# Fewer transposes for the up-projection: four quarters of the sample's rows are transposed, and the four operand sums are formed on the transposed quarters

## The chip, the cores and the metric

The kernel runs on one core of one Trainium2 chip. The metric is the device time of one execution in microseconds; lower is better. Engines are named as the profile names them: PE (TensorE matmul), PEld (its weight load), DVE (VectorE), ACT (ScalarE), POOL (GpSimd) and SP (SyncE, which issues the DMAs). SBUF is the on-chip memory, and PSUM the banks that PE writes its results to.

## What is computed

One encoder layer runs for a prompt of 512 rows and a sample of 1024 rows, with a model width of 1024 and shared weights. The change lies between the output projection and the up-projection of the feed-forward part:

```python
x = x + concat(attention, conv) @ w_out
h = rmsnorm(x, norm_ffn_g)              # (1024, 1024) for the sample
u = dwconv(h @ w_up, ffn_dw_w, ffn_dw_b)  # w_up: (1024, 5632)
x = x + (silu(u[..., :2816]) * u[..., 2816:]) @ w_down
return rmsnorm(x, norm_final_g)
```

## The kernel before

**Seven products.** The sample's up-projection `h @ w_up` is cut into a left and a right half of the model width (L, R), two halves of the rows (t = 0 and 1, 512 rows each) and 22 blocks of columns j. Each j is computed by a scheme of seven products in place of eight. A product is a sum over four chunks c of 128 model dimensions, and a chunk is three matmuls of 128x512, since every fp32 operand is split into a high part (a rounded cast, made by ACT) and a low part (the difference, made by DVE or POOL). In `prod` these are the lines 1194, 1195 (low part of the operand) and 1196 (low part of the weight). The weights' sums and splits are `sums_up` and `split_up` (line 1180, with POOL at line 1074).

**Seven operands.** With e for the rows of t = 0 and x for those of t = 1, the operands on the side of the rows are, by number: 1 is e's left half, 2 is e's right half, 4 is x's right half, 5 is s1 = xL + xR, 6 is s2 = s1 - eL, 7 is eL - xL, and 3 is eR - s2. PE needs them with the model dimensions along the partitions, so rows have to be transposed.

**Rows, sums, transposes.** `scaled(i)` multiplies a finished block of 128 rows by its norm and forms the sums on rows, with DVE. `turned(i, get)` then transposes an operand: for each chunk it takes a bank, runs four transposes of 128x128 (line 1125, one for each block of rows b), casts the high part on ACT (line 1127) and subtracts for the low part on DVE (lines 1128 and 1074). Seven operands of four chunks make 28 banks and 112 transposes. Operands 1 and 2 (32 transposes, banks named "u") are made while the output projection still runs. Operands 4, 6, 7, 5 and 3 (80 transposes) use four banks named "t".

**Order.** PE's order is written by hand from here on (`tc.manual_schedule`); DVE, ACT and POOL are ordered by the scheduler, and each engine executes its list in order. `every(n, gen)` advances the generator of transposes between the chunks of a product, so transposes stand between matmuls in `second(0)`, `fourth(0)` and `second(1)`. A bank "t" is used again when DVE has read it. When the transposes are through, the four banks "t" are given back as two wide banks, "w2" and "w3", for the products' other sums: `armed` writes a throwaway matmul into each (line 1260), ACT copies a first product over it (line 1394), and `sixth(0)` accumulates onto it. Then follow `sixth(1)`, `seventh(0)`, `seventh(1)`, `fifth` and `third`, and the other blocks.

Of the kernel before, what the change touches and what calls it, by code (L numbers as in the profile page):

```python
# [15 lines left out]
P = 128  # L16
D = 1024
# [91 lines left out]
def tile_hybrid_encoder(ctx: ExitStack, tc: tile.TileContext, xs, rel_bias, norm_attn_g, w_in,  # L109
# [981 lines left out]
    def scaled(i):  # L1091
# [3 lines left out]
        if t == 0:  # L1095
            nc.vector.scalar_tensor_tensor(x[:], x1[i][:], rs2[:, i:i + 1], gFb[:], op0=ALU.mult, op1=ALU.mult)
            x1.pop(i)
            return
        for s in (R, L):
            nc.vector.scalar_tensor_tensor(x[:, s], x1[i][:, s], rs2[:, i:i + 1], gFb[:, s], op0=ALU.mult, op1=ALU.mult)  # L1100
        x1.pop(i)
        e = rows[0, b]
        s1 = rows["s1", b] = sb.tile([NT])
        s2 = rows["s2", b] = sb.tile([NT])
        add(s1[:], x[:, L], x[:, R])
        sub(s2[:], s1[:], e[:, L])
        sub(x[:, L], e[:, L], x[:, L])
        if i >= NB - 2:
            last_sum(b)

    def last_sum(b):
        sub(rows[0, b][:, L], rows[0, b][:, R], rows["s2", b][:])

    def block_rows(i, b):
        if i in (1, 2, 3):
            return rows[0, b][:, R if i == 2 else L]
        if i in (4, 7):
            return rows[1, b][:, R if i == 4 else L]
        return rows["s1" if i == 5 else "s2", b][:]

    def turned(i, get):
        for c in range(4):
            held, ap = get()
            for b in range(4):
                nc.tensor.transpose(ap[:, b * P:(b + 1) * P], block_rows(i, b)[:, c * P:(c + 1) * P], ident[:])
            hi, lo = A[i, c] = (sb.tile([NT], F32R), sb.tile([NT], F32R))
            nc.scalar.copy(hi[:], ap)
            sub(lo[:], ap, hi[:].bitcast(F32))
            held = None
            yield 0.0  # L1130
        key = {6: "s2", 5: "s1", 7: 1, 3: 0}.get(i)
        for b in range(4):
            rows.pop((key, b), None)
# [88 lines left out]
    for b in range(2):  # L1222
        last_sum(b)
# [146 lines left out]
    turns = chain(*(turned(i, turn_bank) for i in (4, 6, 7, 5, 3)))  # L1370
# [7 lines left out]
    second(0, every(7, turns))  # L1378
    fourth(0, every(7, turns), True)
    second(1, chain(every(8, turns)))  # L1380
    for _ in turns:
        raise RuntimeError("turns left")
    pt_guard.__exit__(None, None, None)
# [24 lines left out]
    sixth(1)  # L1408
    split_up(1, 3)
# [420 lines left out]
```

## Time and profile before

| what | value |
|---|---|
| median of 3 runs | 1485.77 us (1485.22 to 1486.96) |
| the profiled execution | 1484.85 us, span of its instructions 1483.1 us |
| PE busy | 1468.5 us of the span, 99% |
| DVE, ACT, POOL busy | 1118.2, 805.5 and 770.7 us |
| transposes of `turned` into "u" | 32, from 693.8 to 727.7 us |
| transposes of `turned` into "t" | 80, from 737.8 to 753.3 us |
| first matmul of `sixth(0)` | 757.88 us |

All times of rows are microseconds from the start of the span. A row of the timeline gives start, duration, engine, line, operation, output and inputs by the program's names with numbers left out (w<-h,q), shape and count, and in brackets how long the engine was idle before and what it waited for. Records of matmuls that follow each other overlap; the distance from start to start is what one costs. A group counts as busy from its first start to its last end.

### The profile page before, as it was taken

What the parts mean: (1) busy time and instruction counts of PE and PEld (TensorE: products, weight loads), DVE (VectorE), ACT (ScalarE), POOL (GpSimd) and SP (SyncE); (2) the same over time, 40 slices, a digit from 0 to 9 for tenths busy, and PEclk for the clock granted to TensorE, in tenths of its full rate; (3) what the DMA queues carried; (4) which work ended last, traced back from release to release, by engine and by line L of the source; (5) the groups of instructions that cost most, each with busy time, mean ns of one, the idle gap of its engine ahead of it and who ended that gap; (6) DMA issues with size and microseconds to landing.
All of it is one profiled execution on the core that took longest, in us unless ns stands there. A gap on an engine that the chain in (4) does not pass through costs nothing.

```text
span 1483.1 us, 19870 instructions
## 1 busy us (share of the span) xinstructions
PE 1468.5 (99%) x6736; PEld 1212.0 (82%) x6736; DVE 1118.2 (75%) x1510; ACT 805.5 (54%) x1424; POOL 770.7 (52%) x689
## 2 busy tenths in 40 slices
PE   9999999999999999999999999999999999999998
PEld 7788887878888888788888888888888888888886
DVE  6877945648988888676868888888886856578774
ACT  7524555567778776653465545445544553433355
POOL 3564453338779766322336666666654251135546
PEclk9999999999999999999999999999999999999999
DMA  9554331844444454663214443333332494356644
GB/s 367 200 151 146 102 107 29 263 142 142 127 137 136 134 178 142 201 225 108 71 58 142 135 135 128 127 130 128 123 126 87 152 326 167 124 188 220 224 163 163
DMA packets 124626, 228.19 MB, mean 154 GB/s; under 512 B 20420, under 2 KB 45764, under 8 KB 124397
## 3 DMA queue, kind: packets, MB, share of 16 engines
q1 hardware_dynamic: 124092, 226.37, 46.6%
q8 instruction: 53, 0.87, 0.2%
q10 hardware_dynamic: 432, 0.56, 0.1%
q14 instruction: 49, 0.39, 0.1%
HBM read 166.83 MB, written 61.10 MB: 154 GB/s over the span
## 4 chain that ended last, share of the span: by engine, by line
PE 89%; DVE 3%; DMA 3%; ACT 2%; POOL 2%; issue 1%; SPq 0%; POOLq 0%; DVEq 0%; ACTq 0%
PE w L1194 8%; PE w L1196 8%; PE w L1195 8%; PE w L1528 7%; PE w L1527 7%; PE w L1526 7%; PE b L315 4%; PE b L317 4%; PE b L316 4%; PE u L315 4%; PE u L317 4%; PE u L316 4%; PE a L692 1%; PE a L650 1%; PE u L796 1%; PE u L798 1%
## 5 line engine op out<-in xcount | busy, mean ns | idle before, releaser
L163 POOL TENSOR_TENSOR q<-q,q 128x1024 fp32r<-128x1024 f32 x66 | 159.2, 2412 | 66.9 <-ACT q L162 42.8
L1074 POOL TENSOR_TENSOR q<-q,q 128x512 fp32r<-128x512 f32 x81 | 116.5, 1445 | 119.4 <-ACT q L1180 117.1
L1074 DVE TENSOR_TENSOR h<-h,h 128x512 fp32r<-128x512 f32 (+1 forms) x152 | 131.9, 897 | 57.6 <-ACT h L1082 23.4
L1526 PE MATMUL w<-h,h 128*128 128x512 f32 x432 | 168.0, 389 | 0.0
L1528 PE MATMUL w<-h,h 128*128 128x512 f32 x432 | 168.0, 389 | 0.0
L1527 PE MATMUL w<-h,h 128*128 128x512 f32 x412 | 160.3, 389 | 0.0
L1194 PE MATMUL w<-h,q 128*128 128x512 f32 x368 | 144.3, 392 | 0.7 <-ACT w L1267 0.4
L1196 PE MATMUL w<-h,q 128*128 128x512 f32 x368 | 143.2, 389 | 0.0
L1195 PE MATMUL w<-h,q 128*128 128x512 f32 x347 | 135.0, 389 | 0.0
L1074 POOL TENSOR_TENSOR h<-h,h 128x512 fp32r<-128x512 f32 (+1 forms) x38 | 53.5, 1411 | 142.4 <-ACT h L1509 117.5
L1082 ACT CAST h<-h 128x512 fp32r<-128x512 f32 x116 | 69.3, 620 | 104.4 <-DVE h L1074 25.8
L315 PE MATMUL b<-h,q 128*128 128x512 f32 x312 | 123.0, 395 | 1.4 <-ACT h L461 0.8
L317 PE MATMUL b<-h,q 128*128 128x512 f32 x312 | 122.5, 393 | 0.0
L316 PE MATMUL b<-h,q 128*128 128x512 f32 x312 | 122.3, 392 | 0.0
L315 PE MATMUL u<-h,q 128*128 128x512 f32 x272 | 106.8, 393 | 0.0
L316 PE MATMUL u<-h,q 128*128 128x512 f32 x272 | 106.8, 393 | 0.0
L317 PE MATMUL u<-h,q 128*128 128x512 f32 x272 | 106.7, 392 | 0.0
L162 ACT CAST q<-q 128x1024 fp32r<-128x1024 f32 x66 | 69.1, 1048 | 52.1 <-PE u L316 16.8
L352 DVE SCALAR_TENSOR_TENSOR c<-d,cvw,c 128x512 f32<-128x512 f32 x128 | 96.0, 750 | 1.6
L344 POOL TENSOR_TENSOR h<-h,h 128x512 f32<-128x512 f32 x62 | 81.6, 1318 | 27.5 <-ACT h L343 23.0
L1526 PEld LDWEIGHTS w<-h,h 128*128 128x128 f32 x432 | 81.1, 188 | 16.8
L1528 PEld LDWEIGHTS w<-h,h 128*128 128x128 f32 x432 | 81.1, 188 | 16.7
(474 smaller groups left out, 3990.3 us busy)
## 6 DMA issues: line engine op xcount, KB each, us to landing
q<-in_laid_w_up SPq DMA_DIRECT2D x88, 512.0 KB, 3.7
ga<-q SPq DMA_DIRECT2D x65, 256.0 KB, 2.2
h<-gap SPq DMA_DIRECT2D x57, 256.0 KB, 3.5
h<-ga SPq DMA_DIRECT2D x57, 256.0 KB, 3.5
h<-in_w_down SPq DMA_DIRECT2D x52, 256.0 KB, 3.4
q<-in_laid_w_in SPq DMA_DIRECT2D x22, 512.0 KB, 3.9
gap<-h SPq DMA_DIRECT2D x44, 256.0 KB, 3.2
q<-in_x_sample SPq DMA_DIRECT2D x15, 512.0 KB, 7.5
```

What stands on the lines that cost most here:

```text
L163: (nc.vector if dve else nc.gpsimd).tensor_tensor(lo[:], raw[:], hi[:].bitcast(F32), op=ALU.subtract)
L315: nc.tensor.matmul(out, whi[:, kc, :], hi[:], start=(kc == 0), stop=False)
L316: nc.tensor.matmul(out, whi[:, kc, :], lo[:], start=False, stop=False)
L317: nc.tensor.matmul(out, wlo[:, kc, :], hi[:], start=False, stop=(kc == KC - 1))
L352: nc.vector.scalar_tensor_tensor(acc[:], src(t), w(t), acc[:], op0=ALU.mult, op1=ALU.add)
L1074: (eng or nc.vector).tensor_tensor(out, a, b, op=ALU.subtract)
L1194: nc.tensor.matmul(out, whi[:, s], hi[:], start=(start and c == 0), stop=False, **go)
L1195: nc.tensor.matmul(out, whi[:, s], lo[:], start=False, stop=False, **go)
L1196: nc.tensor.matmul(out, wlo[:, s], hi[:], start=False, stop=(stop and c == 3), **go)
L1526: nc.tensor.matmul(out, sh[:, c], th[:], start=(p == 0 and not seeded), stop=False, **go)
L1527: nc.tensor.matmul(out, sh[:, c], tl[:], start=False, stop=False, **go)
L1528: nc.tensor.matmul(out, sl[:, c], th[:], start=False, stop=(p == NPAIR - 1), **go)
```

## The change

Rows are only scaled; no sum is formed on them. Four quarters are transposed: e left and e right (into "u", by `turned`), x right and x left (into "t", by `turned_second`), 64 transposes in place of 112. For e, ACT copies the transposed bank to SBUF as it is (`turn_raw`), and the high and low parts are made from that copy, the low part on POOL. For x, a chunk takes two banks at once: the right quarter gives operand 4 by its parts; then DVE forms s3 = eL - xL and s2 = xR - s3 from the two banks, and both are held until that is done. s2 is split into operand 6. `last_sums` splits s3 into operand 7, then forms operand 5 (eL + s2) and operand 3 (eR - s2) in place of the raw copies, with DVE, and splits them with ACT and POOL. All transposes into "t" now stand in `second(0)`, 8 behind each of its four chunks.

```diff
--- before.py
+++ after.py
@@ -1092,45 +1092,72 @@
 
         t, b = divmod(i - 4, 4)
         x = rows[t, b] = sb.tile([D])
-        if t == 0:
-            nc.vector.scalar_tensor_tensor(x[:], x1[i][:], rs2[:, i:i + 1], gFb[:], op0=ALU.mult, op1=ALU.mult)
-            x1.pop(i)
-            return
-        for s in (R, L):
+        for s in (R, L) if i >= NB - 2 else (slice(0, D),):
             nc.vector.scalar_tensor_tensor(x[:, s], x1[i][:, s], rs2[:, i:i + 1], gFb[:, s], op0=ALU.mult, op1=ALU.mult)
         x1.pop(i)
-        e = rows[0, b]
-        s1 = rows["s1", b] = sb.tile([NT])
-        s2 = rows["s2", b] = sb.tile([NT])
-        add(s1[:], x[:, L], x[:, R])
-        sub(s2[:], s1[:], e[:, L])
-        sub(x[:, L], e[:, L], x[:, L])
-        if i >= NB - 2:
-            last_sum(b)
-
-    def last_sum(b):
-        sub(rows[0, b][:, L], rows[0, b][:, R], rows["s2", b][:])
-
-    def block_rows(i, b):
-        if i in (1, 2, 3):
-            return rows[0, b][:, R if i == 2 else L]
-        if i in (4, 7):
-            return rows[1, b][:, R if i == 4 else L]
-        return rows["s1" if i == 5 else "s2", b][:]
+
+    turn_raw, sums = {}, {}
+
+    def turn_block(t, c, ap):
+        n, c = divmod(c, 4)
+        for b in range(4):
+            nc.tensor.transpose(ap[:, b * P:(b + 1) * P], rows[t, b][:, n * NT + c * P:n * NT + (c + 1) * P], ident[:])
+
+    def parts_of(i, c, src, eng):
+        hi, lo = A[i, c] = sb.tile([NT], F32R), sb.tile([NT], F32R)
+        nc.scalar.copy(hi[:], src)
+        sub(lo[:], src, hi[:].bitcast(F32), eng)
 
     def turned(i, get):
         for c in range(4):
             held, ap = get()
+            turn_block(0, 4 * (i - 1) + c, ap)
+            raw = turn_raw[i, c] = sb.tile([NT])
+            nc.scalar.copy(raw[:], ap)
+            held = None
+            parts_of(i, c, raw[:], nc.gpsimd)
+            yield 0.0
+        if i == 2:
             for b in range(4):
-                nc.tensor.transpose(ap[:, b * P:(b + 1) * P], block_rows(i, b)[:, c * P:(c + 1) * P], ident[:])
-            hi, lo = A[i, c] = (sb.tile([NT], F32R), sb.tile([NT], F32R))
-            nc.scalar.copy(hi[:], ap)
-            sub(lo[:], ap, hi[:].bitcast(F32))
-            held = None
-            yield 0.0
-        key = {6: "s2", 5: "s1", 7: 1, 3: 0}.get(i)
+                rows.pop((0, b))
+
+    def turned_second(get):
+        for c in range(4):
+            held, right = get()
+            turn_block(1, 4 + c, right)
+            parts_of(4, c, right, None)
+            yield
+            other, left = get()
+            turn_block(1, c, left)
+            if c % 2 == 0:
+                both = sb.tile([2, NT], among="q")
+            s3, s2 = sums[c] = sb.tile([NT]), Part(both, c % 2)
+            sub(s3[:], turn_raw[1, c][:], left)
+            sub(s2[:], right, s3[:])
+            held = other = None
+            parts_of(6, c, s2[:], None)
+            yield
         for b in range(4):
-            rows.pop((key, b), None)
+            rows.pop((1, b))
+
+    def last_sums():
+        for c in range(4):
+            s3, s2 = sums[c]
+            sums[c] = s2
+            parts_of(7, c, s3[:], None)
+            s3 = s2 = None
+        yield
+        for c in range(4):
+            raw = turn_raw.pop((1, c))
+            add(raw[:], sums[c][:], raw[:])
+            parts_of(5, c, raw[:], nc.gpsimd)
+            raw = None
+        yield
+        for c in range(4):
+            raw = turn_raw.pop((2, c))
+            sub(raw[:], raw[:], sums.pop(c)[:])
+            parts_of(3, c, raw[:], nc.gpsimd)
+            raw = None
 
     def old_bank():
         b = bank("turn")
@@ -1219,8 +1246,6 @@
         for half in range(2):
             load_up(j, half)
     drain(side)
-    for b in range(2):
-        last_sum(b)
     split_up(0, 1, 2)
     out_blocks(NB - 2, 0)
     split_up(1, 1, 2)
@@ -1367,7 +1392,7 @@
                 next(gen, None)
             yield
 
-    turns = chain(*(turned(i, turn_bank) for i in (4, 6, 7, 5, 3)))
+    turns = turned_second(turn_bank)
     firsts = []
     for j in range(2):
         st[j] = dict(x=wide())
@@ -1375,11 +1400,14 @@
         a = sb.tile([NT])
         nc.scalar.copy(a[:], st[j]["x"][:, L])
         firsts.append(a)
-    second(0, every(7, turns))
-    fourth(0, every(7, turns), True)
-    second(1, chain(every(8, turns)))
+    second(0, every(8, turns))
     for _ in turns:
         raise RuntimeError("turns left")
+    later = last_sums()
+    next(later)
+    fourth(0, None, True)
+    second(1)
+    next(later)
     pt_guard.__exit__(None, None, None)
     for i in range(2, 4):
         ps2.append(ctx.enter_context(tc.tile_pool(name=f"pw{i}", bufs=1, space=bass.MemoryType.PSUM)))
@@ -1406,6 +1434,7 @@
     sixth(0)
     split_up(0, 3)
     sixth(1)
+    next(later, None)
     split_up(1, 3)
     seventh(0, None, False)
     load_up(3, 0)
```

Where the change moves instructions. A name holds its slot, a running number and a serial number (t2_7 is the seventh tile in "t", in bank t2); `waits` lists the engines and queues on whose semaphores a row waits.

On PE before, each chunk of `fourth(0)` is still followed by 4 or 8 transposes of rows (ident is the identity; t2_11 and t3_12 are chunks 2 and 3 of operand 7, t0_13 the first of operand 5):

```order
L1125 MATMUL t2_11_7710<-ident_82,q3_1208_7229 128x128
L1125 MATMUL t2_11_7710<-ident_82,c2_1231_7402 128x128
L1125 MATMUL t2_11_7710<-ident_82,q8_1246_7468 128x128
L1125 MATMUL t3_12_7719<-ident_82,q10_1189_7115 128x128 [waits DVE_49]
L1125 MATMUL t3_12_7719<-ident_82,q3_1208_7229 128x128
L1125 MATMUL t3_12_7719<-ident_82,c2_1231_7402 128x128
L1125 MATMUL t3_12_7719<-ident_82,q8_1246_7468 128x128
L1194 MATMUL w0_1_7569<-h18_1257_7640,h47_1234_7411 128x512 [waits Activation_49]
L1195 MATMUL w0_1_7569<-h2_1258_7641,h47_1234_7411 128x512
L1196 MATMUL w0_1_7569<-h18_1257_7640,h46_1235_7412 128x512
L1125 MATMUL t0_13_7731<-ident_82,h44_1190_7118 128x128 [waits DVE_49]
```

On PE after, the last group of transposes (t2_7 and t3_8, chunk 3's right and left quarter) stands behind the last matmul of `second(0)`, and `fourth(0)` follows with no transposes between its chunks:

```order
L1223 MATMUL w0_1_7559<-h3_1244_7435,q5_1216_7262 128x512
L1104 MATMUL t2_7_7666<-ident_82,q10_1190_7117 128x128 [waits DVE_49,PE_49]
L1104 MATMUL t2_7_7666<-ident_82,q3_1208_7227 128x128
L1104 MATMUL t2_7_7666<-ident_82,c2_1234_7402 128x128
L1104 MATMUL t2_7_7666<-ident_82,q8_1248_7464 128x128
L1104 MATMUL t3_8_7675<-ident_82,q10_1190_7117 128x128 [waits PE_49]
...
L1221 MATMUL w0_1_7559<-h38_1251_7597,h46_1235_7405 128x512 [waits Activation_49]
L1222 MATMUL w0_1_7559<-h23_1252_7598,h46_1235_7405 128x512
L1223 MATMUL w0_1_7559<-h38_1251_7597,h22_1236_7406 128x512
...
L1221 MATMUL w0_1_7559<-h41_1268_7671,h46_1235_7405 128x512 [waits Activation_49]
L1222 MATMUL w0_1_7559<-h60_1269_7672,h46_1235_7405 128x512 [waits DVE_49]
```

The transposes moved from three products into one; t2_7 reuses the bank of t2_3 and waits for DVE, and the last row waits for DVE's low part of operand 4, chunk 3 (h60).

On DVE before, the stretch of the transposes is one subtraction for each bank, which reads the bank and ACT's high part:

```order
L1074 TENSOR_TENSOR h29_1254_7620<-t1_2_7614,h1_1253_7619 128x512 [waits DMAHW7_49,Activation_49]
L1074 TENSOR_TENSOR h27_1256_7629<-t2_3_7623,h39_1255_7628 128x512 [waits Activation_49]
L1074 TENSOR_TENSOR h2_1258_7641<-t3_4_7635,h18_1257_7640 128x512 [waits Activation_49]
L1074 TENSOR_TENSOR h31_1260_7650<-t0_5_7644,h3_1259_7649 128x512 [waits Activation_49]
L1074 TENSOR_TENSOR h52_1262_7662<-t1_6_7656,h57_1261_7661 128x512 [waits Activation_49]
```

On DVE after, the first eleven (h1 is s3 and q4_1253 s2 of chunk 0, h23 the low part of operand 4, h58 that of operand 7, h11 and h33 the raw copies that become operands 5 and 3, h27 the low part of operand 6):

```order
L1074 TENSOR_TENSOR h1_1254_7607<-h11_1187_7111,t1_2_7601 128x512 [waits PE_49,Activation_49]
L1074 TENSOR_TENSOR h23_1252_7598<-t0_1_7592,h38_1251_7597 128x512 [waits DMAHW5_49,Activation_49]
L1074 TENSOR_TENSOR q4_1253_7606<-t0_1_7592,h1_1254_7607 128x512 [waits DVE_49]
L1074 TENSOR_TENSOR h58_1274_7688<-h1_1254_7607,h55_1273_7687 128x512 [waits Activation_49]
L1074 TENSOR_TENSOR h49_1259_7631<-h14_1203_7208,t3_4_7626 128x512 [waits DMAHW2_49,PE_49]
L1074 TENSOR_TENSOR h2_1258_7623<-t2_3_7617,h43_1257_7622 128x512 [waits DMAHW7_49,Activation_49]
L1071 TENSOR_TENSOR h11_1187_7111<-q4_1253_7606,h11_1187_7111 128x512 [waits DVE_49]
L1074 TENSOR_TENSOR h33_1223_7355<-h33_1223_7355,q4_1253_7606 128x512
L1074 TENSOR_TENSOR h27_1256_7611<-q4_1253_7606,h37_1255_7610 128x512 [waits Activation_49]
L1074 TENSOR_TENSOR h36_1265_7656<-h6_1209_7242,t1_6_7650 128x512 [waits PE_49]
L1074 TENSOR_TENSOR q4_1253_7606<-t2_3_7617,h49_1259_7631 128x512 [waits DVE_49]
```

Chunk 1's s2 (the last row), which ends the use of bank t2, stands behind operands 5 and 3 and the low parts 7 and 6 of chunk 0, all of which read SBUF alone.

On ACT before, the copies into "w2" and "w3" stand behind the last transposes' cast and two casts of weights:

```order
L1127 CAST q13_1289_7808<-t3_20_7803 128x512 [waits PE_49]
L1180 CAST q9_1298_7887<-q7_4_7243 128x512
L1180 CAST c0_1319_8066<-q3_7_7905 128x512 [waits DMAHW2_49,PE_49]
L1394 COPY w2_3_7822<-h24_1249_7582 128x512 [waits PE_49]
L1394 COPY w3_4_7823<-h45_1250_7597 128x512 [waits PE_49]
```

On ACT after, with h13_1281 and h14_1285 the high parts of operand 5, chunks 0 and 2, and h34 that of operand 3, chunk 0:

```order
L1108 CAST h13_1281_7728<-h11_1187_7111 128x512 [waits DVE_49]
L1207 CAST q11_1309_7882<-q12_5_7778 128x512 [waits DMAHW6_49,DVE_49]
L1108 CAST h14_1285_7738<-h6_1209_7242 128x512 [waits Pool_49]
L1422 COPY w2_3_7754<-h24_1249_7572 128x512 [waits PE_49]
L1108 CAST h34_1296_7820<-h33_1223_7355 128x512 [waits PE_49]
L1422 COPY w3_4_7755<-h45_1250_7587 128x512 [waits PE_49]
```

The first copy now stands behind a cast that waits for POOL, and the second behind a cast of operand 3.

## Prediction

> **What bounds the kernel now.** I read the page first (shares of the engines, then the chain that ended last), then what TensorE (PE) waited for, then the stretch in which the changed transposes stand.
>
> ```profile
> span 1483.1 us, 19870 instructions
> PE 1468.5 (99%) x6736; PEld 1212.0 (82%) x6736; DVE 1118.2 (75%) x1510; ACT 805.5 (54%) x1424; POOL 770.7 (52%) x689
> PE 89%; DVE 3%; DMA 3%; ACT 2%; POOL 2%; issue 1%; SPq 0%; POOLq 0%; DVEq 0%; ACTq 0%
> ```
>
> PE is busy 99% and carries 89% of the chain: whatever it is given to do, or made to wait for, is paid in full. The waits of PE from 600 us to the end (total, times, longest):
>
> ```profile
> PE a L706 <- ACT h L694: 1.5, 1, 1.5
> PE w L1194 <- ACT w L1267: 0.4, 1, 0.4
> PE w L1194 <- ACT w L1285: 0.3, 1, 0.3
> PE w L1260 <- DVE q L1074: 0.3, 1, 0.3
> ```
>
> Behind the change only 0.7 us are waited (L1267, L1285), so a shift of PE there arrives at the end almost whole. The transposes of the changed function, and the stretch with the later 80 of them (us; busy of PE, PEld, DVE, ACT, POOL; clock; DMA share; GB/s):
>
> ```profile
> L1125 PE MATMUL t<-ident,q x40: 270/272/273, 737.8 to 753.3; 128*128 128x128 f32 x40
> L1125 PE MATMUL u<-ident,q x32: 270/272/275, 693.8 to 727.7; 128*128 128x128 f32 x32
> L1125 PE MATMUL t<-ident,h x32: 271/272/273, 740.9 to 750.2; 128*128 128x128 f32 x32
> L1125 PE MATMUL t<-ident,c x8: 272/273/273, 738.0 to 747.0; 128*128 128x128 f32 x8
> 737.79:753.36 15.57, 15.57 (x112) 13.85 (x110) 13.83 (x21) 11.05 (x22) 4.01 (x3) 1.00 0.20 69
> ```
>
> There PE never stops, but VectorE (DVE) is busy 13.83 of 15.57 us for 21 instructions. It has little to spare, and the change takes work from PE and gives DVE a longer chain just there.
>
> **What leaves PE.** Before, 80 transposes in eleven gaps, and the ten chunks of 3 product matmuls between them, fill these 15.57 us.
>
> ```profile
> 742.04 1.04 PE L1125 MATMUL t<-ident,h 128*128 128x128 f32 x8
> 742.83 0.47 PE L1194 MATMUL w<-h,h 128*128 128x512 f32 x1
> 743.60 0.60 PE L1125 MATMUL t<-ident,h 128*128 128x128 f32 x4
> 753.36 0.48 PE L1194 MATMUL w<-h,c 128*128 128x512 f32 x1
> 755.96 0.39 PE L1196 MATMUL w<-h,h 128*128 128x512 f32 x1
> 756.61 0.50 PE L1260 MATMUL w<-h 128*128 128x512 f32 x1 [0.26 <-DVE q L1074]
> 757.88 0.41 PE L1194 MATMUL w<-h,h 128*128 128x512 f32 x1
> 879.67 0.39 PE L1194 MATMUL w<-d,q 128*128 128x512 f32 x1
> 879.90 0.39 PE L1195 MATMUL w<-q,q 128*128 128x512 f32 x1
> ```
>
> A product matmul issues every 0.227 us (879.67 to 879.90). Thirty are 6.80 us, so 80 transposes cost 15.57 − 6.80 = 8.77 us, or 0.11 each (not the 0.27 of a single record, which overlaps its neighbours). After the change 32 of the 80 are left: −48 × 0.11 = −5.3 us. The short wait ahead of `armed` goes too (755.96 to 756.61 is 0.65 against a cadence of 0.23): −0.4. A PE that never waits would begin `sixth(0)`, the row at 757.88, at 752.2.
>
> **What the wait on DVE costs.** The four banks "t" hold a left and a right quarter until DVE has read both, for chunk after chunk of 128. DVE executes in order, and its order here is s3 and s2 of a chunk, the low parts of operands 4, 7 and 6, and, already among them, operands 5 and 3: 28 instructions in place of 20 and a few. Their prices:
>
> ```profile
> 740.90 4.65 DVE L1074 TENSOR_TENSOR h<-t,h 128x512 fp32r<-128x512 f32 x7
> 743.00 1.29 POOL L1074 TENSOR_TENSOR q<-h,q 128x512 fp32r<-128x512 f32 x1 [3.77 <-ACT q L1180]
> 748.56 1.89 DVE L1074 TENSOR_TENSOR h<-t,h 128x512 fp32r<-128x512 f32 x3 [0.32 <-ACT h L1127]
> 715.24 0.67 DVE L1074 TENSOR_TENSOR h<-h,q 128x512 f32<-128x512 f32 x1
> 715.84 1.77 DVE L1074 TENSOR_TENSOR q<-q,q 128x512 f32<-128x512 f32 x1
> 717.53 1.77 DVE L778 SCALAR_TENSOR_TENSOR h<-h,h 128x512 f32<-128x512 f32 x1
> 719.23 0.68 DVE L801 TENSOR_TENSOR q<-b,q 128x512 f32<-128x512 f32 x1
> 715.45 3.30 POOL L1074 TENSOR_TENSOR h<-q,h 128x512 fp32r<-128x512 f32 x2 [1.89 <-PE c L797]
> 738.42 0.59 ACT L1127 CAST h<-t 128x512 fp32r<-128x512 f32 x1 [0.53 <-PE t L1125]
> 758.08 0.59 ACT L1394 COPY w<-h 128x512 f32<-128x512 f32 x1 [0.34 <-PE w L1260]
> ```
>
> Alone, one takes 0.69 and the next starts 0.605 later (three in 1.89). Beside GpSimd (POOL) work on SBUF, a DVE instruction with both inputs in SBUF takes 1.77 instead of 0.68: +1.09 (715.84, 717.53). One that reads PSUM isn't slowed: seven from "t" run through a POOL instruction in 4.65 us (740.90).
>
> The Trainium skill, "SBUF — State Buffer", section "SBUF: two separate sides", calls this port pair an exclusive lock held for the whole instruction. The rows agree (1.77 against 0.68, PSUM sources unhurt); by the rule a loser can wait out a whole POOL instruction, 1.29 by the row at 743.00, and five such would add 6.5 us where I take 4.4 below (1493.6 in place of 1491.5).
>
> Now along the order. PE starts the first 8 transposes at 737.79 as before; DVE's first subtraction follows the left quarter's transposes, at 738.86. A group of 8 transposes and 3 matmuls is 743.60 − 742.04 = 1.56, so PE wants groups two to four at 739.35, 740.91 and 742.47.
> 1. The fourth group reuses the bank of chunk 1's right quarter. Its release is s2 of chunk 1, the 11th instruction on DVE: 738.86 + 10 × 0.605 + 0.69 = 745.6, or 746.7 with one blocked. PE stands 3 to 4 us there, and behind it all of `fourth(0)`.
> 2. `fourth(0)` reads the low part of operand 4, chunk 3, the 20th: T = 738.86 + 19 × 0.605 + 0.69 = 751.05, and 1.09 more for each blocked instruction. PE alone would want it at 745.5.
> 3. How many are blocked is what the trace of before can't show. POOL has one low part of a weight behind the cast that stands after chunk 1's on ACT (near 743.2), two more behind the fourth group's first cast, and then operand 3's; at each, DVE has two-input instructions next (low parts 6 and 7, operands 5 and 3: nine of the first 19). Bounds: none (all POOL work meets PSUM readers, as at 740.90) and five. I take four, one per POOL instruction, since each lasts two DVE slots and the two-input ones stand in runs: T = 751.05 + 4.36 = 755.4.
> 4. From T PE has two matmuls left, `second(1)` and `fourth(1)` with 24 and `armed` with 2: 28 × 0.227 and a fill, T + 6.6 = 762.0. But `sixth(0)` needs ACT's copy into its bank, and on ACT that copy now stands behind two casts of operand 5. The first waits for the low part 7 of chunk 3, five DVE slots behind T (T + 3.0); its cast takes 0.6; the second's buffer is released by the second of two POOL subtractions (1.29 to 1.65 each, so T + 6.3 to T + 7.1); a cast and the copy bring T + 7.6 to T + 8.3. PE waits 1.0 to 1.7 more.
>
> So `sixth(0)` starts at 755.4 + 8.3 = 763.7 instead of 757.88: +5.8 us. With none blocked it would be 751.05 + 7.6 = 758.65: +0.8. With five at 1.09, +6.9.
>
> **The rest.** The last row block's scaling before, and the first transposes that read it:
>
> ```profile
> 735.88 0.74 DVE L1100 SCALAR_TENSOR_TENSOR q<-c,rs,q 128x512 f32<-128x512 f32 x1
> 737.79 0.38 PE L1125 MATMUL t<-ident,q 128*128 128x128 f32 x2
> ```
>
> ACT gets 8 instructions more and POOL 16; DVE loses 18, the row sums among them. The 8 raw copies and 8 of POOL's go where the 32 "u" transposes stand (693.8 to 727.7); PE doesn't wait between 690 and 737 at all (of the waits shown, L706's lies at 611), so ACT's 8 × 0.59 and POOL's 8 × 1.65 are hidden by the output projection's matmuls. If that cover were short, the last row block's scale, which POOL also makes, would come late; it is through 1.2 us ahead of the transposes now (736.62 to 737.79), which bounds the loss at perhaps 1 us; I take zero. DVE's freed time in that stretch buys nothing, as PE didn't wait for it. Of operand 5 and 3's low parts, the other eight on POOL, the ones read last are wanted only in `fifth` and `third`, two to four products of 2.7 us (12 × 0.227) later: zero, with about 1 us of margin where `seventh(0)` follows ACT's copy. SP's issues keep their order but for a few weight loads that nothing here waits for.
>
> The sum: −5.7 (PE's own work) + 11.5 (waits) = +5.8 us. The profiled execution took 1484.85 us for its span of 1483.1, 0.9 below the median of 1485.77; its span should become 1488.9, and the median 1491.5.
>
> **Rivals.**
> - *The port is not paid.* DVE's two-input instructions miss POOL's, or only one or two meet: T 751 to 753, `sixth(0)` at 758.7 to 760.8, +0.8 to +2.9: about 1487.3. For it: POOL's four are only 5.2 us of a 12 us chain, and ACT may hold the casts back. Against: the nine instructions in runs. Chance 0.21.
> - *PE's saving arrives whole (faster).* It needs low part 4 of chunk 3 by 746.5 and the fourth group's bank by 743, that is a DVE start every 0.4 us or s2 ahead of the other 14 instructions. Then −5.3 to −5.7: 1480.2. No row shows a DVE step under 0.6 for this shape. It would decide if the chain ended before 747 to 750. Chance 0.05.
> - *PE runs slowly after its waits.* After idling from the start, the first transposes took 0.235 us each, twice the later 0.11, for 3.4 us (1.48 to 4.86; from 5.24 to 5.47 the cadence is 0.23):
>
> ```profile
> 1.48 2.82 PE L246 MATMUL a<-ident 128*128 128x128 f32 x12 [1.48 <-POOL ident masks.py:199]
> 4.86 0.54 PE L526 MATMUL u<-h,h 128*128 128x512 f32 x1
> 5.24 0.40 PE L526 MATMUL b<-h,h 128*128 128x512 f32 x1
> 5.47 0.40 PE L526 MATMUL u<-h,h 128*128 128x512 f32 x1
> ```
>
> Both waits here would be 4 to 5.6 us. After the first, the slower work still ends ahead of T. After the second, PE's 6.6 us from T could grow by half of such a stretch, 1.7, of which the copy's wait hides 1.0 to 1.7; with a wait at `seventh(0)` beside it, +1.5: about 1493. Chance 0.10.
>
> The Trainium skill, "TensorE: Matmul & The Clock Gate", section "What's actually happening", gives half the clock after an idle window of about 3.4 us, until about 3.4 us of work have passed: the same stretch as in the rows, though the profile's clock column shows 1.00 there, and the same 1.7 at most.
>
> **How the numbers follow.** My case has the remaining 0.64. Three runs spread over 1.7 us; 0.2% is 3.0 us, about what a measurement of this kernel can tell from no change, so "same" is 1482.8 to 1488.7: the first rival (0.21) and the lower edge of mine (0.02) fall there. Faster 0.05, slower 0.72. The range goes from no blocking less the runs' spread (1486.6 − 0.8 = 1485.8) to five blocked and the slow clock (1485.77 + 6.9 + 1.5 = 1494.2). Between the two signs the likeliest case's own range is 1489 to 1493.
>
> **What the profile after would show.** Transposes of the changed line into "t": 32, and PE idle before the first of the fourth group, waiting for DVE, 3 to 4 us; idle again before the low-part matmul of `fourth(0)`, 4 to 6 us, for DVE; a third wait of 1 to 2 us at `sixth(0)` for ACT's copy; DVE instructions of about 1.77 us between 742 and 755, four of them; `sixth(0)` at about 763.7; later matmuls shifted by the same amount. If PE's waits sum to about 6 us, the port was not paid; if the first wait is missing, DVE is quicker than its rows or the banks come free earlier than I read; if something after 765 waits, the operands 5 and 3 from POOL are late.

## The result, and the profile after

| | time, us | span, us |
|---|---|---|
| before, five runs | 1485.77 (1485.22 to 1486.96) | 1483.1 |
| changed, five runs | 1511.89 (1508.94 to 1513.67) | 1508.9 |

The ratio is 1.0172 (95% interval 1.0158 to 1.0187): the change makes the kernel 26 us slower. I forecast 1491.5, with 1494.2 as the upper end. The page of the changed kernel:

```profile
span 1508.9 us, 19846 instructions
PE 1472.4 (98%) x6688; PEld 1208.1 (80%) x6688; DVE 1085.3 (72%) x1492; ACT 809.9 (54%) x1432; POOL 777.5 (52%) x705
PE 74%; DVE 10%; DMA 5%; issue 5%; ACT 4%; POOL 1%; SPq 0%; POOLq 0%; ACTq 0%; DVEq 0%
```

PE has 48 instructions less and yet PE's share of the chain fell from 89% to 74%: DVE (10%), DMA (5%) and ACT (4%) now decide parts of it. The waits of PE from the first transposes into "t" to the down-projection (total, times, longest):

```profile
PE w L1221 <- ACT w L1292: 12.1, 15, 1.7
PE t L1104 <- DVE q L1074: 4.1, 1, 4.1
PE w L1222 <- DVE h L1074: 2.6, 1, 2.6
PE w L1221 <- ACT w L1422: 1.8, 1, 1.8
PE w L1221 <- DVE q L1339: 1.0, 3, 0.4
PE w L1221 <- DVE w L1071: 0.5, 1, 0.5
```

The three waits of the transposes' stretch are there (L1104, L1222, L1422). What I had not expected is the first row, 15 waits in the loop over the blocks j, for ACT's copy of the first product into the second sum's bank (line 1292, in `first`). Cut into stages, with starts from PE's rows:

| stage, us | before | changed |
|---|---|---|
| up to the first transpose into "t" | 737.8 | 738.7 |
| from there to `sixth(0)` | 20.1 | 25.0 |
| from `sixth(0)` to the first matmul of the down-projection | 399.2 | 419.2 |
| the rest | 326.0 | 326.1 |

Of the 25.8 us, 0.9 lie ahead of the stretch (the first "u" transposes, too, start 1.0 later, 694.8 for 693.8, with nothing changed ahead of them; in the runs below they start between 692.6 and 695.0), 4.9 in it, and 20.0 in the loop behind it. But for the parts of operands 5 and 3 at its start, the change does not touch the loop's instructions. Behind the start of `sixth(0)` the listed waits are 13.6 us (0.7 before), and 1.7 us go to a slow clock there (below). Most of what is left of the 20.0 goes with the restarts, since a listed wait leaves out part of what it costs: by the PE rows below some 0.27 us, for 19 waits an estimated 5 us.

What ACT's activations at the start of each convolution (`dwconv`, line 1312 before and 1337 after; one for the gate half and one for the value half of each block) wrote to before, and what ended the idle time ahead of them:

```profile
L1312 ACT ACTIVATE q<-w,vecs,fw x26: 1191/1208/1212, 767.8 to 1175.0; 128x1024 f32<-128x1024 f32 x26
L1312 ACT ACTIVATE c<-w,vecs,fw x18: 1192/1208/1214, 788.0 to 1111.1; 128x1024 f32<-128x1024 f32 x18
...
DMA ga<-q: 3.1, 1
```

and after:

```profile
L1337 ACT ACTIVATE q<-w,vecs,fw x43: 1191/1209/1217, 775.2 to 1200.6; 128x1024 f32<-128x1024 f32 x43
L1337 ACT ACTIVATE c<-w,vecs,fw x1: 1200/1200/1200, 792.2 to 792.2; 128x1024 f32<-128x1024 f32 x1
DMA ga<-q: 26.0, 8
```

Before, 18 results went into a slot "c"; after, one. And eight activations waited 26.0 us for a store of an earlier result (ga<-q) to leave the slot that they were to write. The chain of one such wait, on ACT:

```profile
895.40 1.21 ACT L1337 ACTIVATE q<-w,vecs,fw 128x1024 f32<-128x1024 f32 x1 [3.76 <-DMA ga<-q]
...
900.76 1.21 ACT L1337 ACTIVATE q<-w,vecs,fw 128x1024 f32<-128x1024 f32 x1
...
904.72 0.57 ACT L1292 COPY w<-w 128x512 f32<-128x512 f32 x1 [2.24 <-DVE q L1339]
```

and on PE:

```profile
904.69 0.39 PE L1223 MATMUL w<-h,q 128*128 128x512 f32 x1
905.34 0.50 PE L1221 MATMUL w<-h,q 128*128 128x512 f32 x1 [0.26 <-ACT w L1292]
905.68 0.40 PE L1222 MATMUL w<-h,q 128*128 128x512 f32 x1
```

The gate half waits for the store, the value half comes late behind it, DVE's convolution (L1339) still reads the bank that ACT's copy (L1292) is to write, and PE waits for the copy. This wait of PE is one of the short ones (the longest is 1.7 us). It counts as 0.26 us, but the two starts come 0.65 and 0.34 us behind the ones before them in place of 0.23: 0.53 us lost, 0.27 more than listed.

The reason lies in the program's own allocator. `Slots.tile` hands out the smallest size that fits, and of that size the slot that has been free longest:

```python
least = min(s[1] for s in fits)
slot = next(s for s in fits if s[1] == least)
```

The sizes are "h" (61 of 2048 bytes), "d" (2 of 2304), "q" (15 of 4096) and "c" (4 of 4352). The 56 parts of the operands stay for the whole loop. They lay in 51 "h", 3 "q" and 2 "d" before, and lie in 54 "h" and 2 "d" after. So the loop has three more "q" and three fewer "h". The slots free when the value half of block 4 begins:

```
before:   h24 h49 h21 h34 h33 c0 h40 c1
changed:  c2 c0 c3 h16 h33 h50 c1 q8
```

Before, no "q" is free, and the tile of 4096 bytes goes into a long idle "c". After, one "q", the one given back last, is free; it is smaller than a "c", so 21 of the 22 value halves take a "q", and the "c" lie idle.

### The profile page after: what moved, and what is told of

Same layout as the page of the kernel before. It is cut to its first block, busy times and chain, and to the rows that moved or that the text cites. A ratio compares the mean times of both kernels' runs of the same rounds, so it can differ in the third digit from the quotient of the medians.

```text
span 1508.9 us, 19846 instructions
## 1 busy us (share of the span) xinstructions
PE 1472.4 (98%) x6688; PEld 1208.1 (80%) x6688; DVE 1085.3 (72%) x1492; ACT 809.9 (54%) x1432; POOL 777.5 (52%) x705
## 4 chain that ended last, share of the span: by engine, by line
PE 74%; DVE 10%; DMA 5%; issue 5%; ACT 4%; POOL 1%; SPq 0%; POOLq 0%; ACTq 0%; DVEq 0%
PE w L1557 7%; PE w L1556 7%; PE w L1555 7%; PE b L315 4%; PE b L316 4%; PE b L317 4%; PE w L1221 4%; PE w L1222 4%; PE w L1223 4%; PE u L315 4%; PE u L317 4%; PE u L316 4%; DVE q L1074 3%; DMA ga<-q 3%; DVE q L1339 2%
## 5 line engine op out<-in xcount | busy, mean ns | idle before, releaser
L1074 POOL TENSOR_TENSOR q<-q,q 128x512 fp32r<-128x512 f32 x118 | 165.7, 1410 | 159.8 <-ACT q L1207 133.1
L1221 PE MATMUL w<-h,q 128*128 128x512 f32 x560 | 220.6, 394 | 13.6 <-ACT w L1292 12.1
L1223 PE MATMUL w<-h,q 128*128 128x512 f32 x560 | 218.0, 389 | 0.0
L1222 PE MATMUL w<-h,q 128*128 128x512 f32 x516 | 201.0, 390 | 0.0
L1074 DVE TENSOR_TENSOR h<-h,h 128x512 fp32r<-128x512 f32 (+1 forms) x156 | 128.7, 852 | 55.6 <-ACT h L1082 22.5
L1556 PE MATMUL w<-h,h 128*128 128x512 f32 x412 | 160.3, 389 | 0.0
L1074 POOL TENSOR_TENSOR h<-h,h 128x512 fp32r<-128x512 f32 (+1 forms) x52 | 72.9, 1404 | 153.8 <-ACT h L1538 124.1
L1221 PEld LDWEIGHTS w<-h,q 128*128 128x128 f32 x560 | 105.1, 188 | 44.2 <-ACT w L1292 18.5
L1223 PEld LDWEIGHTS w<-h,q 128*128 128x128 f32 x560 | 105.1, 188 | 22.2
L1222 PEld LDWEIGHTS w<-h,q 128*128 128x128 f32 x516 | 96.9, 188 | 19.2
L1338 DVE SCALAR_TENSOR_TENSOR q<-w,fw,q 128x1023 f32<-128x1023 f32 x43 | 55.0, 1280 | 72.7 <-ACT q L1337 71.5
L1207 ACT CAST q<-q 128x512 fp32r<-128x512 f32 x118 | 73.0, 621 | 47.2 <-DVE q L1074 20.2
```

The lines of the kernel that those rows point to most:

```text
L1074: (eng or nc.vector).tensor_tensor(out, a, b, op=ALU.subtract)
L1207: nc.scalar.copy(hi[:], src)
L1221: nc.tensor.matmul(out, whi[:, s], hi[:], start=(start and c == 0), stop=False, **go)
L1222: nc.tensor.matmul(out, whi[:, s], lo[:], start=False, stop=False, **go)
L1223: nc.tensor.matmul(out, wlo[:, s], hi[:], start=False, stop=(stop and c == 3), **go)
L1556: nc.tensor.matmul(out, sh[:, c], tl[:], start=False, stop=False, **go)
```

## Experiments

Theory S (slots): the loop's 20 us come from this choice of slot. Rival B (backlog): DVE comes late out of the stretch of transposes and the loop, where it has little to spare, never gains it back.

### The value half in "c"

```diff
-        u = sb.tile([W2])
+        u = sb.tile([W2], among="c" if f >= NJ and any(x[0][0] == "c" for x in sb.free) else None)
```

> The changed kernel, with one edit: the tile of the value half's convolution is taken from the four wide slots "c" when one is free, as the kernel before happens to do. Slot theory (behind sixth(0) the change loses its 20 us because three more slots "q" are free, so that the allocator, which takes the smallest slot that fits, hands out the one "q" that was just given back and leaves all four "c" idle): ACT's activation of the value half no longer waits, PE's waits for ACT's copy of the first product (12.1 us in 15) fall under 3 us, the stretch from the first to the last of these copies goes from 376 us to 360 to 365, and the time from 1511.9 to about 1496 (1493 to 1500). Backlog theory (DVE is late after the transposes and never catches up, whatever the slots): 1510 to 1513, with the same 15 waits.

Measured: 1490.38 us (1488.43 to 1492.72), ratio to before 1.0031 (1.0020 to 1.0041). PE's waits from the transposes to the down-projection:

```profile
PE t L1104 <- DVE q L1074: 4.1, 1, 4.1
PE w L1222 <- DVE h L1074: 3.6, 1, 3.6
PE w L1221 <- DVE w L1071: 0.5, 1, 0.5
```

and where ACT's activations went:

```profile
L1337 ACT ACTIVATE q<-w,vecs,fw x22: 1207/1207/1212, 773.2 to 1177.5; 128x1024 f32<-128x1024 f32 x22
L1337 ACT ACTIVATE c<-w,vecs,fw x22: 1187/1208/1212, 785.7 to 1179.1; 128x1024 f32<-128x1024 f32 x22
```

All 15 waits are gone, and from `sixth(0)` to the down-projection it takes 398.0 us (before 399.2, changed 419.2). One choice of slot is worth 21.5 us; the stretch of the transposes is even longer than in the changed kernel (26.9 us for 25.0), and the loop is repaired all the same, so B falls. It came out below the range expected: from the first to the last of ACT's copies it takes 355.8 us, where I had expected 360 to 365 (before 359.9, changed 375.3). What is left, +4.7 us, is a loss in the stretch alone, as I had forecast it (+5.8): in the profiled execution the stretch is 6.8 us longer than before, and an earlier start (736.5) and the shorter loop give 2.4 of them back.

### The operands in the slots of before

```diff
-        hi, lo = A[i, c] = sb.tile([NT], F32R), sb.tile([NT], F32R)
+        hi, lo = A[i, c] = (sb.tile([NT], F32R, among="q" if (i, c) == (3, 3) else None),
+                            sb.tile([NT], F32R, among="q" if i == 3 and c > 1 else None))
```

> The changed kernel, with the last three parts of operand 3 put into slots "q", where the kernel before has three parts of its last two chunks: the slots left for the loop are then the same in kind as before (6 "q", 4 "c", 10 "h"). Slot theory: the loop runs at 360 us again, 1494 to 1499. Backlog theory: 1510 to 1513.

Measured: 1499.92 us (1499.78 to 1500.07), ratio 1.0091 (1.0076 to 1.0106). Of PE's waits for ACT's copy of the first product (L1293 here) 0.4 us are left:

```profile
PE w L1222 <- ACT h L1302: 3.9, 1, 3.9
...
PE w L1556 <- DVE q L1340: 2.1, 1, 2.1
...
PE w L1222 <- ACT w L1293: 0.4, 1, 0.4
```

From the first to the last of these copies it takes 359.4 us, as S expected. The time lies 1 us above what I expected: ACT's copy behind `sixth` (L1302) now comes late, 3.9 us once, and so does a convolution of DVE that the down-projection waits for (L1556), 2.1 us once. From `sixth(0)` to the down-projection are 406.4 us, with 6.5 us of waits, and the rest takes 330.0 us in place of 326.0.

### The kernel before, with three "c" taken away

```diff
-            hi, lo = A[i, c] = (sb.tile([NT], F32R), sb.tile([NT], F32R))
+            hi, lo = A[i, c] = (sb.tile([NT], F32R, among="c" if (i, c) == (3, 3) else None),
+                                sb.tile([NT], F32R, among="c" if i == 3 and c > 1 else None))
```

> The kernel before, all 112 transposes and its own order, with the same three parts put into slots "c" in place of "q": the loop then has 9 "q" and 1 "c", and one just returned "q" is taken for the value half, as in the changed kernel. Slot theory: 8 to 16 us slower than before, 1494 to 1502, with waits of PE for ACT's copy of the first product. Backlog theory: nothing in the stretch of the transposes has changed, so 1485.8 within 1 us.

Measured: 1521.65 us (1520.38 to 1523.51), ratio 1.0238 (1.0223 to 1.0253), more than twice what I had expected. PE's longest waits:

```profile
PE w L1195 <- ACT w L1268: 16.9, 8, 2.1
PE w L1195 <- DVE q L1315: 8.1, 7, 1.6
```

and ACT's activations (line 1313 here), with what they waited for:

```profile
L1313 ACT ACTIVATE q<-w,vecs,fw x43: 1202/1208/1214, 768.9 to 1213.4; 128x1024 f32<-128x1024 f32 x43
L1313 ACT ACTIVATE c<-w,vecs,fw x1: 1212/1212/1212, 785.4 to 785.4; 128x1024 f32<-128x1024 f32 x1
DMA ga<-q: 25.5, 7
```

The kernel before, with all its transposes and a stretch of 20.4 us, shows the same picture: 43 results in "q", one in "c", 25.5 us of waits for stores, and a loop of 436.7 us. (Three "c" are occupied here, where in the changed kernel they lie idle; in both the value half falls back on a "q".) Where three of 56 tiles lie is enough to make it, without the change. Part of why it is more than expected is PE's clock: behind five of the waits, each of about 2.1 us, it was at 0.50 for 3.4 us (the first from 821.1 to 824.5), half of which, 8.5 us in all, is lost.

### DVE in the order of the program

```diff
-    second(0, every(8, turns))
+    with tc.manual_schedule(engines={mybir.EngineType.PE, mybir.EngineType.DVE}):
+        second(0, every(8, turns))
...
```

> The changed kernel, with DVE's instructions in the stretch of the transposes kept in the order of the program (the sums of a chunk and its low parts first, operand 7's low parts and operand 5 behind them); nothing is done about the slots. The low part of operand 4, chunk 3, is then the 16th instruction of DVE in place of the 20th: sixth(0) starts at 757 to 760 in place of 763.7. Slot theory: the loop behind still takes 376 us, so 1505 to 1509. Backlog theory: DVE is in time, the loop goes back to 360 us, 1486 to 1492.

Measured: 1515.27 us (1513.57 to 1516.18), slower than the changed kernel. PE's waits up to 790 us:

```profile
PE w L1221 <- ACT h L1301: 4.4, 1, 4.4
PE w L1222 <- DVE h L1074: 3.9, 1, 3.9
PE t L1104 <- DVE q L1074: 1.5, 1, 1.5
```

The wait for the bank fell from 4.1 to 1.5 us and the stretch from 25.0 to 21.9 us; `sixth(0)` came at 760.5, 0.5 later than expected. But ACT's copy behind `sixth` (L1301) came late, 4.4 us, and the loop kept its loss (427.9 us), with 15 waits for ACT's copy of the first product (12.2 us). DVE is earlier out of the stretch, and the loop gains nothing by it: against B.

### An order by hand on DVE and ACT

The next two put DVE's and ACT's instructions of the stretch in an order by hand, the first with the value half in "c" as above (the edit in part):

```diff
-            parts_of(4, c, right, None)
+            hi, lo = A[4, c] = sb.tile([NT], F32R), sb.tile([NT], F32R)
+            nc.scalar.copy(hi[:], right)
...
             sub(s2[:], right, s3[:])
+            sub(lo[:], right, hi[:].bitcast(F32))
             held = other = None
-            parts_of(6, c, s2[:], None)
...
     def last_sums():
+        for c in range(4):
+            parts_of(6, c, sums[c][1][:], None)
...
+    hand = tc.manual_schedule(engines={mybir.EngineType.PE, mybir.EngineType.DVE, mybir.EngineType.Activation})
...
     sixth(0)
+    next(later)
     split_up(0, 3)
```

Operand 4's low part stands right behind s2, operand 6 is split in `last_sums`, and operand 5 behind `sixth(0)`.

With the value half in "c":

> The changed kernel with the edit of the first run (value half in a slot "c") and the stretch of the transposes in an order by hand on DVE and ACT: s3, s2 and the low part of operand 4 for each chunk first, then the low parts of 6 and 7; operand 5 is split behind sixth(0) and operand 3 behind sixth(1); ACT's copies into the wide banks stand ahead of both, and POOL has no low part of a weight to make meanwhile. The low part of operand 4, chunk 3, is DVE's 12th instruction: 738.86 + 11 x 0.605 + 0.69 = 746.2 by the clock of the profile before, where PE wants it at 745.5, and the bank that stopped PE for 4.1 us is free at 742.0, ahead of need. If DVE's order and its port are what cost the first stretch its 11 us: waits of PE there under 2 us in all, sixth(0) at 752.5 to 754.5 (15 to 16.5 us behind the first transpose into "t", 25.0 with the change), no slow matmuls, and 1479 to 1483 in all, faster than before. Rival: the low parts of operand 5, moved back behind four of weights on POOL, come late for fifth(0), which is 10.9 us behind sixth(0); then a new wait of 2 to 4 us there and 1482 to 1487.

Without:

> The same order by hand as in the run beside it, with nothing done about the slots. If the two losses are separate, the first stretch is as short as there, and the loop behind it still pays some 20 us (419 us from sixth(0) to the first product of the down-projection, 398.9 before): 1499 to 1504. If they are one (the loop pays because DVE comes late out of the first stretch), 1479 to 1486.

Measured: 1510.49 us (1509.95 to 1511.87) with "c", and 1545.87 (1544.23 to 1549.06) without. The first half of the expectation held: the stretch takes 15.7 us in both, with 0.7 us of waits and no slow matmul, 4.4 less than before the change. DVE's order, POOL beside it and ACT's order make up the local loss together; these runs do not tell them apart. The rest fell: the first lies 27 us above its range, the second over 40. Behind the stretch PE waited 21.3 us in the one with "c":

```profile
PE w L1224 <- ACT h L1317: 8.8, 1, 8.8
PE w L1226 <- POOL q L1074: 6.6, 7, 0.9
PE w L1224 <- ACT h L1304: 2.9, 7, 0.5
PE w L1224 <- ACT h L1325: 2.5, 1, 2.5
```

ACT ahead of the copy that the first of these names:

```profile
772.02 0.62 ACT L1108 CAST h<-h 128x512 fp32r<-128x512 f32 x1 [4.97 <-POOL h L1074]
```

The 8.8 us are ACT's copy behind `seventh`, which stands behind a cast of operand 3 that waits for POOL, and around the end of this wait PE's clock was at 0.50, from 770.0 to 776.8. The loop loses again: 428.3 us, and 463.1 without "c", where ACT waits for stores 7 times (21.0 us). I had held the slots for settled, and the new order had moved them once more: all 56 parts of the operands lie in "h", and 5 "h" and the two "d" are left. That this is what the rest of the loop's loss comes from is not shown: with the first run's 7 "h" the loop had as many small slots and took 398.0 us.

The third of these, by hand and with three parts in "q":

> The order by hand, with the last three parts of operand 3 in slots "q" (the slots of the kernel before) in place of the value half in "c". Slot theory: the loop takes about 399 us as before, 1480 to 1485. If the wide slots "c" mattered for another reason than how many "q" are free, the loop stays above 405 us.

Measured: 1489.93 us (1487.62 to 1490.96), ratio 1.0028 (1.0019 to 1.0038). The loop waits 3.8 us in all and takes 404.3 us, between the 399 of S and the 405 named against it. The time lies 5 us above the range, with a wait of 3.0 us for ACT's copy behind `seventh` and one of 2.0 us in the down-projection.

### The late low parts on DVE

The sums and low parts of operands 5 and 3 on DVE, and the places of operand 3's last parts named, so that the slots left are known: 54 "h" and 2 "d" in the first, 51 "h", 3 "q" and 2 "d" in the second. This run and all that follow keep the order by hand and the value half in "c"; "slots of before" says only where the operands' parts lie (the edit in part).

```diff
-            parts_of(5, c, raw[:], nc.gpsimd)
...
+                parts_of(i, c, raw[:], None)
...
+        put = {(3, 2): (None, "d"), (3, 3): (None, "d")}.get((i, c), (None, None))
+        hi, lo = A[i, c] = [sb.tile([NT], F32R, among=k or "h") for k in put]
```

The first:

> The changed kernel, the order by hand of the runs before, and the low parts of operands 5 and 3 on DVE (idle by then) in place of POOL, with the sums of both made right behind the low parts of 7; two parts of operand 3 in the two slots "d" and all other operands in "h", so that the loop finds 4 "c", 3 small "h" and one "q" free, as in the first run; the value half in "c". The late copies on ACT for fifth(0) and seventh(0) (8.8 us of PE in the run by hand, where ACT stood behind POOL's low parts) should be gone: sixth(0) at about 754, waits of PE from there to the down-projection under 2 us, 397 us from sixth(0) to its first product as in the first run, 326 behind that: span 1477 to 1479, time 1479 to 1483, faster than before by 3 to 6 us. If the loop's loss comes from the order and not from the slots, over 1500.

The second:

> The same, with three parts of operand 3 in "q" and two in "d", so that the slots left for the loop are those of the kernel before (10 "h", 6 "q", 4 "c"). Slot theory: 399 us from sixth(0) to the first product of the down-projection, as before: 1481 to 1485, some 2 us behind the run beside it.

Measured: 1491.52 us (1490.22 to 1493.91) and 1487.47 (1486.18 to 1488.55), ratio 1.0011 (1.0003 to 1.0020) for the second. Both lie above their ranges, by 8.5 and 2.5 us. The loop fell to 404.9 and 405.1 us. The 4 us between the two lie behind it (329.9 and 326.0 us): in the first the down-projection waits 2.1 us for a convolution of DVE, and PE's clock is at 0.50 for 3.4 us after it. In the second, ACT's last cast of operand 5 waited for POOL, whose two low parts of weights took 6.0 us beside DVE's low parts, and PE waited 2.7 us for the copy behind it:

```profile
755.83 6.00 POOL L1074 TENSOR_TENSOR q<-h,q 128x512 fp32r<-128x512 f32 x2 [16.80 <-ACT q L1213]
760.64 0.62 ACT L1109 CAST h<-h 128x512 fp32r<-128x512 f32 x1 [2.79 <-POOL q L1074]
```

### POOL's low parts where POOL is idle

The splits of operand 7's weights (and, in the last run, those of 5) stand ahead of the low parts of 6 and 7:

```diff
+    split_up(0, 7)
+    split_up(1, 7)
     later = last_sums()
```

With the slots of before:

> The run with low parts on DVE and the slots of before (1487.5), with one move more: the split of operand 7's weights, whose low parts POOL took 6.0 us to make beside DVE and for which ACT's last cast of operand 5 waited, stands ahead of the low parts of 6 and 7, where POOL is idle. The wait of seventh(0) for ACT's copy (2.7 us) and the slow matmuls behind it (1.6 us) should go: 1482.5 to 1484.5, faster than the kernel before. If another cast holds ACT in its place, 1486 to 1488.

With 54 "h" and 2 "d", as in the first run of the section before:

> The same move on the run with the value half in "c" (1491.5): its 3.6 us of waits for ACT's copy and the slow matmuls behind them go, the 2.1 us ahead of the down-projection stay: 1485 to 1488. With the slots of before beside it, it tells whether one returned "q" still costs anything once the value half has the "c": if so it is 2 to 4 us behind.

And with both splits early, slots of before:

> The last but one run (low parts on DVE, slots of before, split of operand 7's weights early: 1485.8), with the split of operand 5's weights moved early as well, so that POOL makes these two low parts where it is idle (748 to 757) and not beside DVE's low parts of operands 5 and 3, which took 1.7 us each there. DVE reaches the sum behind seventh(0) some 4 us earlier, so that the convolution of the first gate half and ACT's copy behind it come in time: the 2.5 us at fifth(1) and the slow matmuls behind it (1.5 us) go, 1481.5 to 1483.5, faster than the kernel before. If the earlier low parts block DVE ahead of sixth(0) instead, a wait of 1 to 2 us appears there and 1484 to 1486.

Measured: 1485.80 us, ratio 1.0005 (0.9996 to 1.0014); 1488.31, 1.0016 (1.0007 to 1.0024); and 1485.54, 0.9999 (0.9990 to 1.0008). The first and the last, which I had expected to be faster than the kernel before, are as fast; none is faster. The second has the same wait in the down-projection as the first run of the section before (the rest takes 329.9 us, 326.0 in the other two). PE's waits in the last run, from the transposes to the down-projection:

```profile
PE w L1227 <- ACT h L1307: 2.3, 2, 1.5
PE w L1227 <- ACT w L1316: 0.7, 1, 0.7
PE w L1228 <- DVE h L1074: 0.5, 1, 0.5
```

Each move took away the wait that it was made for and left a smaller one behind it. The stretch is 15.7 us for 20.1 before, and 4.0 us of these 4.4 are given back between `sixth(0)` and the down-projection (403.1 for 399.2), where 3.7 us are waited: PE comes 4 us earlier to the next products, and ACT's copies do not. The longest of these waits is a matter of slots once more. ACT's copy behind `sixth(0)`, for which PE waits 1.5 us,

```profile
759.72 0.59 ACT L1307 COPY h<-w 128x512 f32<-128x512 f32 x1 [2.44 <-DVE h L1074]
```

takes the "h" that the raw copy of operand 5's chunk 0 has just given back. DVE's low part of that chunk, which stands behind the sums of operand 3, still has to read it, and the copy waits 2.44 us. The next one (0.8 us) stands behind casts of operand 3 that wait for DVE. Whether another slot for the first would make the kernel faster than before was not tried.

## Why the prediction was wrong, point by point

**What held.** The local part of the sum came out as worked, its times to the tenth by luck. `sixth(0)` started at 763.69 (forecast 763.7), the low part of operand 4, chunk 3, let PE go at 755.22 (755.4), and three waits stand where they were named. PE's rows of the changed kernel behind the three waits:

```profile
747.75 0.66 PE L1104 MATMUL t<-ident,q 128*128 128x128 f32 x2 [4.11 <-DVE q L1074]
755.22 0.50 PE L1222 MATMUL w<-h,h 128*128 128x512 f32 x1 [2.61 <-DVE h L1074]
763.69 0.50 PE L1221 MATMUL w<-h,h 128*128 128x512 f32 x1 [1.82 <-ACT w L1422]
```

The blocked ones on DVE:

```profile
744.65 1.75 DVE L1074 TENSOR_TENSOR h<-q,h 128x512 fp32r<-128x512 f32 x1
750.52 1.77 DVE L1074 TENSOR_TENSOR h<-h,h 128x512 fp32r<-128x512 f32 x1
752.22 1.75 DVE L1074 TENSOR_TENSOR h<-q,h 128x512 fp32r<-128x512 f32 x1
```

Three instructions were blocked, not four; the 1.09 us for the fourth were made up by a start 0.9 us later, two misses that cancel. The first run's +4.7 us, with the loop repaired, is about this part by itself, against +5.8. That the order of DVE and ACT and POOL's work beside DVE set it, taken together, is shown from the other side by the order by hand: 15.7 us with 0.7 of waits. DVE's order alone brought 21.9.

**The step that failed** is the sentence "so a shift of PE there arrives at the end almost whole", and with it "zero" for all that lies behind. I priced instructions, waits and engines, and took the loop behind for unchanged since its instructions were. Its tiles weren't in the same slots. The rows at 879.67 and 879.90, which I quoted for PE's cadence, read operands from "d" and "q" (w<-d,q and w<-q,q), and the names in the new order say which slots the operands take after. I read in it who waits for whom within the stretch, and not which slots it leaves behind. In its place the runs show a loop that takes 20.0 us more, of the 25.8 in all: ACT's activations wait 26.0 us for stores to leave a "q", and with the value half in a "c" the loop is back at 398.0 us. About 18 of the 20.0 are this mis-step, and 1.7 the slow clock below, which I had put inside the third wait.

**The second wait** was 2.6 us, not 4 to 6, because PE came to it late: it was at half its clock (below) for the first 3.0 us behind the first one. The end of the wait, which counts, was right.

**The rivals.** "The port is not paid" fell (three rows of 1.75 us). "PE's saving arrives whole" is what the runs by hand come near to for the stretch alone (4.4 us of the 5.7), with s2 ahead as that rival asked. (The shortest DVE step of this shape in the trace of before is 0.575 us, not 0.6, far from the 0.4 that it named.) "PE runs slowly after its waits" was real, and the clock column shows it, as it did not at the start of the kernel (us; busy of PE, PEld, DVE, ACT, POOL; clock):

```profile
747.75:750.77 3.02, 3.02 (x12) 2.73 (x13) 3.02 (x6) 2.46 (x5) 0.72 (x1) 0.50 0.00 0
764.50:767.83 3.33, 3.33 (x10) 2.56 (x9) 0.00 (x0) 0.79 (x2) 2.93 (x3) 0.51 0.00 0
```

The first was hidden by the wait for T, as said. The second followed the wait at `sixth(0)` and cost 3.33 / 2 = 1.7 us, which I had let that wait hide; it came behind it, in the loop's share of the table.

**What would have shown it.** I had written that a wait after 765 would mean late operands 5 and 3. It came, and it meant something else: the first row of PE's waits names line 1292, and ACT's idle time names the store.

## What to carry to other kernels

When a change alters what stays in memory, list where each long-lived tile lies and what is free afterwards, as you list instructions: 3 tiles of 56 moved 20 us. An allocator that takes the smallest fit can reuse the slot whose store is still under way while larger ones lie idle; let a tile that is written next choose among all that have been free for long (tried here for one tile, the value half). And an engine that is released earlier gains only as much as the engines behind it are early too: here 4.4 us were won on PE, and 4.0 of them were lost again in the products behind.

## What the runs showed of the hardware

PE went to a clock of 0.50 for about 3.4 us also behind short waits. In the run with operand 7's weights early (1485.80 us), PE waited 2.52 us; 1.0 us after it started again (771.96) the matmuls became slow:

```profile
770.92 0.50 PE L1227 MATMUL w<-h,q 128*128 128x512 f32 x1 [2.52 <-ACT h L1320]
...
771.96 0.62 PE L1228 MATMUL w<-h,q 128*128 128x512 f32 x1
```

and the window from there has the clock at 0.50:

```profile
771.96:775.14 3.18, 3.18 (x9) 2.50 (x8) 3.18 (x5) 2.17 (x2) 0.00 (x0) 0.50 0.00 0
```

The Trainium skill, "TensorE: Matmul & The Clock Gate", section "What's actually happening", gives the slow clock after an idle window of about 3.4 us. The length of the slow stretch agrees (in this run the clock column has 0.50 over the 3.41 us from 771.95 on); the wait ahead of it was shorter here, 2.52 us, so that a gap under that length is not safe. In the kernel before, even a wait of 1.49 us (ended at 627.56) was followed by a clock of 0.50 from 629.62 to 633.03; in the last run a wait of 1.79 us at the same place was not. In the first run PE was slow from 746.4 to 749.8 and again from 754.1, after a wait of 3.6 us, to 760.1; there a matmul starts every 0.43 us.

POOL loses to DVE as DVE does to POOL: two low parts took 6.0 us beside runs of DVE instructions with two inputs in SBUF (755.83 in the run with the late low parts on DVE), against 1.29 us for one beside DVE instructions that read PSUM (743.00 before the change).
